# A hybrid decoder layer on one core: conditioning chunks and sample outputs in quarters of TensorE's array, another order of the first loads, and multiplies of unused data at the start

## The chip, the cores and the metric

The kernel runs on one core of a Trainium2 chip. The metric is the device time of one execution in microseconds, as the median of several runs. The core has a matrix engine (TensorE, PE in the rows; PEld is its weight load), VectorE (DVE), ScalarE (ACT), GpSimd (POOL) and SyncE (SP), and 16 DMA engines that serve queues. Each engine runs its own instructions in the order in which they stand in the program and waits on semaphores for the others.

## The reference

One decoder layer works on a prompt of 1024 tokens and on 8 samples of 4 tokens each, 1024 features, all in fp32. What matters here are three parts of it (shortened):

```python
mod = silu(c) @ ada_w + ada_b             # c: 9 vectors (1 prompt, 8 samples); ada_w 1024 x 6144
sh1, sc1, gt1, sh2, sc2, gt2 = split(mod, 6)
h = rmsnorm(x, norm1_g) * (1 + sc1) + sh1
u = h @ w_in                              # projections of all branches
...
# GLA branch, four heads, each with a state S of 128 x 256 per sequence
att = einsum('bhik,bhjk,bhijk->bhij', q, k, decay)
o = einsum('bhij,bhjv->bhiv', att, v) + einsum('bhik,bhkv->bhiv', q * exp(bc), S)
...
x = x + gt1 * (m @ w_out)                 # then the FFN, with sh2, sc2, gt2
```

The conditioning vectors `mod` scale and shift the normed inputs and gate the sums. They are needed for 9 sequences only, but their matrix has 6 million weights (24 MB).

## The kernel before

Activations lie transposed, features on the 128 partitions and tokens along the free axis. The work goes in two halves: half A has 512 prompt tokens, half B the other 512 and the 32 sample tokens. Every projection is done as three fp32r matmuls per 128 features of depth (`gemm`, L358 to L360): weights and activations are split into a high and a low part, and high x high, high x low, low x high are summed. So each weight tile of 512 KB is loaded by SP into a raw buffer and split by a cast on ScalarE and a subtraction on VectorE (`load_w`, L125 and L126), with three raw and three split buffers. The list scheduler of the framework decides at build time in which order each engine gets its instructions; it follows the order of the code, priorities, and the releases of pool buffers. A pool named `S` of 17 buffers holds whole activations and loads, two PSUM banks (`ax`) serve small results, six the projections.

The conditioning matrix is worked off in 12 chunks of 512 columns (`cc`), each of four loads of 512 KB, two depth tiles of 128 features in each. Its stationary operand is the activated conditioning matrix `cth`, which has 9 used columns of 32. Chunks 2 and 0 give the scale and shift of the first four feature tiles, chunks 3 and 1 those of the others, chunks 4 to 11 are needed later.

Chunks 2, 0, 3 and 1 go through `ada_first`: fp32 matmuls of 32 output columns, each to one of four groups of 32 output partitions (`g`, L178); a copy of the result (`row`, L181); and four matmuls by a selection matrix `sel`, which add the four groups and transpose them (L184). An fp32 matmul is recorded as two, one for each of its passes. 2 and 0 stand after the sum of squares of the first norm (`nps`, L365) and the spread of its result over the partitions (`rps`, L377). 3 and 1 stand between the halves of the norm, after the projection `lrps` and four projections `early20` to `early25` have done their first four feature tiles.

Chunks 4 to 11 go through `ada_chunk`: loads by `load_w` with the split, 16 fp32r matmuls on the full array (L226) whose stationary operand `cst` has the high part in columns 0 to 8 and the low part in 32 to 40 (`ada_split`, with the tile `zz`), a copy of 41 rows, four transposes of 41 columns (L198), two VectorE operations that add the parts. They are woven into the projections of half A up to about 500 us.

In half B each of four GLA heads computes the output of the samples, `pos`: eight fp32 matmuls (one per sample, L751) and one of the attention within the samples (L752) are summed in output partitions 0 to 31, copied to `osb`, turned by two transposes, and copied by ScalarE into the output tile.

Names that recur: `atta` is the product of attention weights (VectorE, L602) from the PSUM tile `dpsa`; `rpsoa` spreads a norm over partitions (L377); `rpsa`, `kpsa`, `vpsa`, `qpsa` are projections of half A.

Of the kernel before, what the change touches and what calls it, by code (L numbers as in the profile page):

```python
# [11 lines left out]
OP = mybir.AluOpType  # L12
PSUM = bass.MemoryType.PSUM
# [33 lines left out]
def hybrid_layer(ctx, tc, I, O):  # L47
# [42 lines left out]
    pool.dma_start(lmask, I["lmask"])  # L90
    bmask = cp.tile([P, NB], F32, name="bmask")
    pool.dma_start(bmask, I["bmask"])
    sel = cp.tile([P, 9], F32, name="sel")
    pool.dma_start(sel, I["sel"])
    hlru0 = cp.tile([P, NR, NB], F32, name="hlru0")
    pool.dma_start(hlru0, I["slru"])
    sconv = cp.tile([P, NR, NB, 3], F32, name="sconv")
    pool.dma_start(sconv, I["sconv"])
# [70 lines left out]
    def ada_first(cc):  # L169

        ps = ax(f"adaps{cc}")
        for kk in range(4):
            raw = S(f"ada{cc}{kk}")
            sp.dma_start(raw[:, :1024], I["ada_w"][cc, kk])
            for i in range(2):
                kt = 2 * kk + i
                g = 32 * (kt % 4)
                pe.matmul(ps[g:g + 32, :], cth[:, kt, :], raw[:, i * 512:(i + 1) * 512], start=(kt < 4), stop=(kt >= 4))  # L178
            yield 1.0
# [3 lines left out]
        for i in range(4):  # L183
            pe.matmul(tps[:, i * 16:i * 16 + 9], row[:, i * P:(i + 1) * P], sel, start=True, stop=True)  # L184
        mo = mod[:, 4 * cc:4 * cc + 4, :]
        dve.scalar_tensor_tensor(mo, tps[:, :64].rearrange("p (j m) -> p j m", m=16)[:, :, 0:9], 0.5, ada_bias(cc),
                                 op0=OP.mult, op1=OP.add)
        ada_derive(cc, mo)
        yield 1.0

    def ada_bias(cc):
        return bc(vec[:, V_ADAB + 4 * cc:V_ADAB + 4 * cc + 4].unsqueeze(2), [P, 4, 9])

    def ada_out(cc, ps, tps, row):
        n = 41
        act.activation(row[:n, :512], ps[:n], AF.Copy)
        for i in range(4):
            pe.transpose(tps[:, i * 64:i * 64 + n], row[:n, i * P:(i + 1) * P], ident[:n, :n])  # L198
        t3 = tps[:, :256].rearrange("p (j m) -> p j m", m=64)
        mo = mod[:, 4 * cc:4 * cc + 4, :]  # L200
        dve.scalar_tensor_tensor(mo, t3[:, :, 0:9], 0.5, ada_bias(cc), op0=OP.mult, op1=OP.add)
        dve.scalar_tensor_tensor(mo, t3[:, :, 32:41], 0.5, mo, op0=OP.mult, op1=OP.add)
        ada_derive(cc, mo)


    cst = []

    def ada_split():
        zz = S("zz")
        pool.memset(zz, 0.0)  # L210
        cw = S("cst", F32R)
        dve.tensor_copy(cw, zz)
        c3 = cw[:, :KD * P].rearrange("p (k m) -> p k m", m=P)
        dve.tensor_copy(c3[:, :, 0:9], cth[:, :, 0:9])
        dve.tensor_sub(c3[:, :, 32:41], cth[:, :, 0:9], c3[:, :, 0:9].bitcast(F32))
        cst.extend(c3[:, i, :] for i in range(KD))

    def ada_chunk(cc):

        ps = ax(f"adaps{cc}")  # L220
        for kk in range(4):
            w = load_w(I["ada_w"][cc, kk], 1024, f"ada{cc}{kk}")
            for i in range(2):
                kt = 2 * kk + i
                for u in range(2):
                    pe.matmul(ps, cst[kt], w[:, u, i * 512:(i + 1) * 512], start=(kt == 0 and u == 0),  # L226
                              stop=(kt == KD - 1 and u == 1))
            yield 0.87
        yield 0.5
        ada_out(cc, ps, ax(f"adat{cc}"), T(f"adar{cc}"))  # L230
# [89 lines left out]
    class Half:  # L320
# [129 lines left out]
        def norm1(s):  # L450
            box = s.rb1
            s.h = []
            for q in range(2):
                if s.hf == 0 and q:
                    s.lr_half(0)
                    for i, t in enumerate((T_Q, T_Q + 1, T_K, T_K + 1)):
# [4 lines left out]
                    for cc in (3, 1):  # L461
                        yield from ada_first(cc)
# [102 lines left out]
        def gla(s, pr, z, q, k, vg, vts):  # L565
# [125 lines left out]
            for i in range(2):  # L691
# [33 lines left out]
                if s.hf:  # L725
# [39 lines left out]
                    for v in range(2):  # L765
                        pe.transpose(pot[:, v * NS:(v + 1) * NS], osb[:, v * P:(v + 1) * P], ident[:NS, :NS])
# [494 lines left out]
```

## Time and profile before

| | us |
|---|---|
| median of three runs | 2069.88 (2068.68 to 2071.18) |
| profiled execution, its own time | 2071.19 |
| its span, from first to last instruction | 2069.4 |
| TensorE busy in the span | 2022.4 |
| VectorE busy | 1132.5 |
| ScalarE busy | 831.5 |
| mean granted TensorE clock (1 is 2.4 GHz) | 0.993 |

The span ends with the last instruction; 1.8 us of the profiled execution lie outside it. The table by stages says how much of a stretch each engine was busy. In a timeline each row is a run of equal operations; the number in brackets is the engine's idle time ahead of it and what ended that.

### The profile page before, as it was taken

The page shows a single profiled execution, that of the slowest core. Times are in us where ns is not written, and L with a number is a line of the kernel's source. Part 1 is how long each engine was busy: PE and PEld are TensorE (multiplying, and loading weights), DVE is VectorE, ACT ScalarE, POOL GpSimd, SP SyncE. Part 2 cuts the span into 40 slices and gives each one's busy share as a digit, 9 for nine tenths or more (in the row PEclk, how much of TensorE's full clock was granted, in tenths as well). Part 3 has the DMA queues.
Part 4 walks back from the last instruction along what each step waited for, and adds up shares of the span by engine and source line. Part 5 has one row for each costly group of instructions (what it writes and reads, how often), then busy time and mean ns, then how long its engine had stood idle before and what let it go on. Part 6 is the DMA issues. An engine that isn't in the chain of part 4 may idle for free. (4 is left out here: it accounts for less than half of the span.)

```text
span 2069.4 us, 31495 instructions
## 1 busy us (share of the span) xinstructions
PE 2022.4 (98%) x13106; PEld 1835.9 (89%) x13106; DVE 1132.5 (55%) x1795; ACT 831.5 (40%) x1153; POOL 85.3 (4%) x136
## 2 busy tenths in 40 slices
PE   6999999999999999999999999999999999999997
PEld 4787887788899888888899898899999999999997
DVE  4757767655347433446564597684243673333356
ACT  3536456645235322233352345563232442212232
POOL 1101001000000000000010011110000000000000
PEclk9999999999999999999999999999999999999999
DMA  7233423433344423342422313322233542232234
GB/s 284 79 111 94 138 76 116 134 122 110 98 154 148 133 79 105 102 139 72 152 69 85 115 48 105 107 78 96 79 96 99 166 136 94 75 107 86 90 114 126
DMA packets 74270, 228.39 MB, mean 110 GB/s; under 512 B 8496, under 2 KB 16304, under 8 KB 74128
## 3 DMA queue, kind: packets, MB, share of 16 engines
q1 hardware_dynamic: 70960, 216.98, 32.6%
q0 software_dynamic: 2624, 8.85, 1.2%
q8 instruction: 103, 1.69, 0.3%
q10 hardware_dynamic: 544, 0.56, 0.1%
q14 instruction: 39, 0.32, 0.0%
HBM read 217.12 MB, written 9.23 MB: 109 GB/s over the span
## 5 line engine op out<-in xcount | busy, mean ns | idle before, releaser
L360 PE MATMUL f3psb<-fab,f3b_hl 128*128 128x272 f32 x352 | 101.4, 288 | 0.0
L358 PE MATMUL f3psb<-fab,f3b_hl 128*128 128x272 f32 x352 | 101.3, 288 | 0.0
L359 PE MATMUL f3psb<-fab,f3b_hl 128*128 128x272 f32 x352 | 100.9, 287 | 0.0
L125 ACT ACTIVATE f3b_hl<-f3b_raw 128x768 fp32r<-128x768 f32 (+1 forms) x45 | 35.7, 793 | 88.4 <-PE f3psb L360 56.1
L358 PE MATMUL f3psa<-faa,f3a_hl 128*128 128x512 f32 x176 | 68.7, 390 | 0.0
L360 PE MATMUL f3psa<-faa,f3a_hl 128*128 128x512 f32 x176 | 68.5, 389 | 0.0
L359 PE MATMUL f3psa<-faa,f3a_hl 128*128 128x512 f32 x176 | 68.5, 389 | 0.0
L358 PEld LDWEIGHTS f3psb<-fab,f3b_hl 128*128 128x128 f32 x352 | 66.4, 189 | 0.0
L360 PEld LDWEIGHTS f3psb<-fab,f3b_hl 128*128 128x128 f32 x352 | 66.2, 188 | 0.0
L359 PEld LDWEIGHTS f3psb<-fab,f3b_hl 128*128 128x128 f32 x352 | 66.1, 188 | 0.0
L126 DVE TENSOR_TENSOR f3b_hl<-f3b_raw,f3b_hl 128x768 fp32r<-128x768 f32 (+1 forms) x45 | 40.1, 892 | 35.1 <-ACT f3b_hl L125 34.9
L125 ACT ACTIVATE f3a_hl<-f3a_raw 128x768 fp32r<-128x768 f32 (+1 forms) x32 | 25.4, 793 | 84.2 <-PE f3psa L360 46.4
L126 DVE TENSOR_TENSOR ada_hl<-ada_raw,ada_hl 128x1024 fp32r<-128x1024 f32 x32 | 38.9, 1222 | 24.8 <-ACT ada_hl L125 24.6
L126 DVE TENSOR_TENSOR f3a_hl<-f3a_raw,f3a_hl 128x768 fp32r<-128x768 f32 (+1 forms) x32 | 28.5, 890 | 39.0 <-ACT f3a_hl L125 38.3
L125 ACT ACTIVATE ada_hl<-ada_raw 128x1024 fp32r<-128x1024 f32 x32 | 33.5, 1054 | 35.6 <-PE vpsa L360 13.1
L358 PE MATMUL uxpsb<-h1b,uxpsb_hl 128*128 128x272 f32 x160 | 47.4, 296 | 0.0
L360 PE MATMUL uxpsb<-h1b,uxpsb_hl 128*128 128x272 f32 x160 | 46.2, 289 | 0.0
L358 PE MATMUL ugpsb<-h1b,ugpsb_hl 128*128 128x272 f32 x160 | 46.2, 289 | 0.0
L359 PE MATMUL uxpsb<-h1b,uxpsb_hl 128*128 128x272 f32 x160 | 46.1, 288 | 0.0
L360 PE MATMUL ugpsb<-h1b,ugpsb_hl 128*128 128x272 f32 x160 | 46.0, 288 | 0.0
L359 PE MATMUL ugpsb<-h1b,ugpsb_hl 128*128 128x272 f32 x160 | 45.8, 286 | 0.0
L360 PEld LDWEIGHTS f3psa<-faa,f3a_hl 128*128 128x128 f32 x176 | 33.0, 188 | 7.1 <-DVE f3a_hl L126 0.2
(1491 smaller groups left out, 7248.5 us busy)
## 6 DMA issues: line engine op xcount, KB each, us to landing
ada_raw<-in_ada_w SPq DMA_DIRECT2D x32, 512.0 KB, 3.6
f3b_raw<-in_ffn SPq DMA_DIRECT2D x23, 384.0 KB, 3.1
ada<-in_ada_w SPq DMA_DIRECT2D x16, 512.0 KB, 10.0
f3b_raw<-in_ffn SPq DMA_DIRECT2D x22, 320.0 KB, 2.9
woa_raw<-in_w_out SPq DMA_DIRECT2D x13, 512.0 KB, 3.4
wob_raw<-in_w_out SPq DMA_DIRECT2D x13, 512.0 KB, 3.3
f3a_raw<-in_ffn SPq DMA_DIRECT2D x16, 384.0 KB, 3.1
uxpsa_raw<-in_w_in SPq DMA_DIRECT2D x10, 512.0 KB, 3.6
```

The lines of the kernel that those rows point to most:

```text
L125: act.activation(hl[:, 0, :n], raw[:, :n], AF.Copy)
L126: dve.tensor_sub(hl[:, 1, :n], raw[:, :n], hl[:, 0, :n].bitcast(F32))
L358: pe.matmul(out, wh, x[:, o:o + w], start=st, stop=False)
L359: pe.matmul(out, wh, x[:, N + o:N + o + w], start=False, stop=False)
L360: pe.matmul(out, wl, x[:, o:o + w], start=False, stop=en)
```

## The change

All 12 chunks now go through one `ada_chunk`. A chunk is done in two halves of two loads; in each, four fp32 matmuls go to the four groups of output partitions, one depth tile each. The loads go straight into buffers of the pool `S`, with no split. The row copy has 128 rows, four full 128x128 transposes by the identity follow, and a VectorE reduction adds the four groups. `sel`, `zz`, `cst` and `ada_split` are gone.

The sample output `pos` is written in the same way: sample `b` goes to group `b % 4`, the attention part to group 96 to 127; `osb` has 128 rows, the two transposes are 128x128, and a VectorE reduction takes the place of ScalarE's last copy.

The loads of the masks and states (`lmask` 224 KB, `bmask` 4, `hlru` 40, `sconv` 120) leave GpSimd's queue at the start and stand in SP's queue after `early25`; the load of `sel` (4.5 KB) is gone. The loads of chunk 3 move ahead of `early24`, those of chunk 1 ahead of the matmuls of chunk 3. The function `occupy` multiplies unused data: ten fp32 matmuls of 128x512 zeros (set by a GpSimd memset) before the first norm's sums, and single ones around chunks 2 and 0.

```diff
-    pool.dma_start(lmask, I["lmask"])
-    pool.dma_start(bmask, I["bmask"])
-    pool.dma_start(sel, I["sel"])
-    pool.dma_start(hlru0, I["slru"])
-    pool.dma_start(sconv, I["sconv"])
+    def load_later():
+        for t, src in (lmask, "lmask"), (bmask, "bmask"), (hlru0, "slru"), (sconv, "sconv"):
+            sp.dma_start(t, I[src])
...
+    def groups(t, n):
+        return t.rearrange("p (j g m) -> p j m g", g=4, m=32)[:, :, 0:n, :]
...
+    def ada_chunk(cc, raws=None):
+        ps = ax(f"adaps{cc}")
+        for kk in range(0, 4, 2):
+            two = raws[kk:kk + 2] if raws else ada_load(cc, kk, kk + 2)
+            for g in range(4):
+                pe.matmul(ps[32 * g:32 * g + 32, :], cth[:, 2 * kk + g, :], two[g // 2][:, (g % 2) * 512:(g % 2 + 1) * 512],
+                          start=(kk == 0), stop=(kk == 2))
             yield 1.0
         row = T(f"adar{cc}")
         act.activation(row[:, :512], ps, AF.Copy)
         tps = ax(f"adat{cc}")
         for i in range(4):
-            pe.matmul(tps[:, i * 16:i * 16 + 9], row[:, i * P:(i + 1) * P], sel, start=True, stop=True)
+            pe.transpose(tps[:, i * P:(i + 1) * P], row[:, i * P:(i + 1) * P], ident)
         mo = mod[:, 4 * cc:4 * cc + 4, :]
+        dve.tensor_reduce(mo, groups(tps, 9), axis=AX.X, op=OP.add)
...
+                        if i == 2:
+                            a3 = ada_load(3, 0, 4)
...
-                    for cc in (3, 1):
-                        yield from ada_first(cc)
+                    a1 = ada_load(1, 0, 4)
+                    yield from ada_chunk(3, a3)
+                    yield from ada_chunk(1, a1)
...
                     for b in range(NB):
-                        pe.matmul(pos[:NS, :256], qm[:, b, :], sts[b // 4][:, (b % 4) * 256:(b % 4 + 1) * 256], start=(b == 0), stop=False)
-                    pe.matmul(pos[:NS, :256], atts[:, i * NS:(i + 1) * NS], vs[0], start=False, stop=True)
+                        g = 32 * (b % 4)
+                        pe.matmul(pos[g:g + 32, :256], qm[:, b, :], sts[b // 4][:, (b % 4) * 256:(b % 4 + 1) * 256], start=(b < 4),
+                                  stop=(3 < b < 7), skip_group_check=True)
+                    pe.matmul(pos[96:128, :256], atts[:, i * NS:(i + 1) * NS], vs[0], start=False, stop=True, skip_group_check=True)
...
-                        pe.transpose(pot[:, v * NS:(v + 1) * NS], osb[:, v * P:(v + 1) * P], ident[:NS, :NS])
-                    act.activation(o3[:, :, HP:], pot[:, :2 * NS].rearrange("p (v j) -> p v j", v=2), AF.Copy)
+                        pe.transpose(pot[:, v * P:(v + 1) * P], osb[:, v * P:(v + 1) * P], ident)
+                    dve.tensor_reduce(o3[:, :, HP:], groups(pot[:, :256], NS), axis=AX.X, op=OP.add)
...
+    zero = S("zero")
+    pool.memset(zero, 0.0)
+    idle = mm("idle")[:, 0]
+    def occupy(src, n):
+        for _ in range(n):
+            pe.matmul(idle, src[:, :P], src[:, :512], start=True, stop=True, skip_group_check=True)
+    occupy(zero, 10)
     A.load_x()
-    drain(A.norm1_sum())
-    drain(ada_first(2))
-    drain(ada_first(0))
+    a2, a0 = ada_load(2, 0, 4), ada_load(0, 0, 4)
+    sums = A.norm1_sum()
+    next(sums)
+    drain(ada_chunk(2, a2))
+    occupy(a2[3], 1)
+    drain(sums)
+    occupy(a0[1], 1)
+    drain(ada_chunk(0, a0))
+    occupy(a0[3], 2)
     drain(A.norm1())
-    ada_split()
+    load_later()
```

The scheduler then gives the engines new orders. Each row below is a run of equal instructions with its line, output and inputs.

TensorE at the start of the program, before (`ada20` to `ada23` are the four loads of chunk 2, `adat2` its turned result):

```order
L365 MATMUL nps1a_147<-ones_93,acc1a_117 128x1 x4
L365 MATMUL nps1a_147<-ones_93,sq1a7_145 128x1 x4
L377 MATMUL rps1a_170<-ident_80,rstd1a_156 128x128 x4
L178 MATMUL adaps2_177<-ada20_178,cth_107 32x512 x2
L178 MATMUL adaps2_177<-ada21_182,cth_107 32x512 x2
L178 MATMUL adaps2_177<-ada22_186,cth_107 32x512 x2
L178 MATMUL adaps2_177<-ada23_190,cth_107 32x512 x2
L184 MATMUL adat2_196<-sel_86,adar2_194 128x9 x4
L178 MATMUL adaps0_203<-ada00_204,cth_107 32x512 x2
L178 MATMUL adaps0_203<-ada01_208,cth_107 32x512 x2
L178 MATMUL adaps0_203<-ada02_212,cth_107 32x512 x2
L178 MATMUL adaps0_203<-ada03_216,cth_107 32x512 x2
```

and after:

```order
L1116 MATMUL idle_113<-zero_111 128x512 x10
L334 MATMUL nps1a_170<-ones_87,acc1a_124 128x1 x4
L334 MATMUL nps1a_170<-ones_87,sq1a7_152 128x1 x4
L186 MATMUL adaps2_193<-ada20_154,cth_101 32x512 x2
L186 MATMUL adaps2_193<-ada21_156,cth_101 32x512 x2
L186 MATMUL adaps2_193<-ada22_158,cth_101 32x512 x2
L186 MATMUL adaps2_193<-ada23_160,cth_101 32x512 x2
L1116 MATMUL idle_113<-ada23_160 128x512
L193 MATMUL adat2_204<-ident_80,adar2_202 128x128 x4
L346 MATMUL rps1a_213<-ident_80,rstd1a_179 128x128 x4
L186 MATMUL adaps0_221<-ada00_162,cth_101 32x512 x2
L1116 MATMUL idle_113<-ada01_164 128x512
```

The multiplies of unused data stand first, chunk 2 stands ahead of the spread `rps1a`, and single multiplies stand inside chunk 0 and (in the rows that follow) before and behind its transposes. The projection `lrpsa` follows as it did.

TensorE where chunk 5 begins, among projections of half A, before:

```order
L360 MATMUL vpsa101_1081<-h1a1_236,vpsa101_hl_1084 128x512
L198 MATMUL adat4_1030<-ident_80,adar4_1031 128x41 x4
L226 MATMUL adaps5_1040<-ada50_hl_1043,cst_410 128x512 x4
L705 MATMUL upsa000_1054<-va00_527,kta0_619 128x256
L358 MATMUL vpsa101_1081<-h1a2_241,vpsa101_hl_1084 128x512
L359 MATMUL vpsa101_1081<-h1a2_241,vpsa101_hl_1084 128x512
L360 MATMUL vpsa101_1081<-h1a2_241,vpsa101_hl_1084 128x512
```

and after:

```order
L186 MATMUL adaps5_946<-ada50_947,cth_101 32x512 x2
L620 MATMUL spsa02_955<-wa02_877 128x64 x5
L186 MATMUL adaps5_946<-ada51_949,cth_101 32x512 x2
L620 MATMUL spsa02_955<-wa02_877 128x64 x3
L328 MATMUL kpsa11_967<-h1a5_410,kpsa11_hl_970 128x512
L329 MATMUL kpsa11_967<-h1a5_410,kpsa11_hl_970 128x512
```

Before, the four matmuls of a load form one piece. After, the two of a load stand alone here, with five matmuls of another product between them and the next two. The eight chunks form 17 such pieces: four of two matmuls in chunk 4; two, two and four in chunks 5 and 6; eight at once in 7, 9 and 11; four and four in 8 and 10. The loads of chunk 4 stand in SP's queue between those of the projections `vpsa`. In `pos`, three heads have two pieces, four matmuls and then four with the attention part; one head has one.

VectorE around 175 to 190 us, where TensorE has its longest wait in mid-program, for the product `atta1` of the tile `dpsa11` (`kea1`, `wa` and `oa` are products of the attention, `rpsa1_hl` the split of a weight), before:

```order
L588 TENSOR_TENSOR kea1_1301<-bca1_1226 128x1024
L602 TENSOR_TENSOR atta1_1307<-dpsa10_1308,ident_80 128x512
L126 TENSOR_TENSOR rpsa1_hl_1409<-rpsa1_raw_1407,rpsa1_hl_1409 128x1024
L632 TENSOR_TENSOR wa164_1396<-bca1_1226 128x8x64
L633 TENSOR_TENSOR wa164_1396<-bca1_1226 128x8x64
L795 TENSOR_TENSOR oa00_1128<-oa00_1128,rboa00_1319 128x1024
L602 TENSOR_TENSOR atta1_1307<-dpsa11_1322,ident_80 128x512
```

and after:

```order
L195 TENSOR_REDUCE mod_98<-adat6_1301 128x36
L560 TENSOR_TENSOR kea1_1311<-bca1_1235 128x1024
L196 SCALAR_TENSOR_TENSOR mod_98<-mod_98,vec_78 128x36
L574 TENSOR_TENSOR atta1_1317<-dpsa10_1318,ident_80 128x512
L209 TENSOR_TENSOR shd_100<-mod_98 128x32
L125 TENSOR_TENSOR rpsa2_hl_1483<-rpsa2_raw_1481,rpsa2_hl_1483 128x1024
L769 TENSOR_TENSOR oa00_1138<-oa00_1138,rboa00_1329 128x1024
L574 TENSOR_TENSOR atta1_1317<-dpsa11_1332,ident_80 128x512
```

Before, four operations stand between the two products `atta1`; after, the first of them stands behind the reduction of chunk 6 and `kea1`, and three stand between the two. On TensorE the second spread, `rpsoa01`, waited for the second `atta1`; now it waits for ScalarE's copy of the first spread `rpsoa00`, which waits for the reduction, and `dpsa11` behind them waits for the first `atta1`. Three projection matmuls lie between `rpsoa00` and `dpsa11`.

## Rows read from the trace of the kernel before

**Rows 1.** The page's first part: busy us, share of the span, instructions.

```profile
PE 2022.4 (98%) x13106; PEld 1835.9 (89%) x13106; DVE 1132.5 (55%) x1795; ACT 831.5 (40%) x1153; POOL 85.3 (4%) x136
```

**Rows 2.** Table by stages: us, busy us by engine, PEclk, DMA, GB/s.

```profile
0.00:60.00 60.00, 38.03 (x184) 25.42 (x185) 27.16 (x79) 19.83 (x30) 5.86 (x17) 0.93 0.71 259
...
190.00:520.00 330.00, 330.00 (x1529) 267.46 (x1528) 216.74 (x293) 183.23 (x241) 18.55 (x29) 0.99 0.36 115
```

**Rows 3.** TensorE's waits: who waits for whom, us in total, times, longest.

```profile
PE nps1a L365 <- DVE lw L270: 13.5, 1, 13.5
```

**Rows 4.** Timeline of PE, the start: start us, us, operation [idle before].

```profile
13.51 1.84 PE L365 MATMUL nps1a<-ones,acc1a 128*128 128x1 f32 x8 [13.51 <-DVE lw L270]
...
19.27 2.07 PE L377 MATMUL rps1a<-ident,rstd1a 128*128 128x128 f32 x8 [2.22 <-DVE rstd1a L289]
21.27 3.31 PE L178 MATMUL adaps<-ada,cth 128*32 128x512 f32 x16
...
26.33 1.92 PE L178 MATMUL adaps<-ada,cth 128*32 128x512 f32 x16
...
32.06 0.77 PE L479 MATMUL lrpsa<-h1a,lr_hla 128*128 128x512 f32 x1 [2.00 <-DVE lr_hla L474]
```

**Rows 5.** Table by stages, of four short stretches.

```profile
13.00:17.00 4.00, 3.50 (x16) 3.49 (x16) 0.61 (x3) 0.00 (x0) 0.00 (x0) 1.00 1.03 415
34.00:36.00 2.00, 2.00 (x6) 1.54 (x5) 2.00 (x3) 1.28 (x3) 0.00 (x0) 0.50 0.67 252
38.00:40.00 2.00, 2.00 (x11) 1.64 (x10) 0.84 (x1) 1.06 (x1) 0.00 (x0) 1.00 0.72 258
188.00:195.00 7.00, 6.41 (x22) 5.49 (x22) 6.00 (x9) 3.28 (x6) 0.19 (x1) 0.51 0.07 5
```

**Rows 6.** Timeline of the other engines, the start.

```profile
1.98 0.56 POOL L90 DMA_DIRECT2D lmask<-in_lmask  x1
...
12.68 0.68 DVE L393 TENSOR_TENSOR acc1a<-acc1a,sq1a 128x512 f32<-128x512 f32 x1
...
28.31 1.00 POOL L210 MEMSET zz<- 128x1088 f32 x1 [22.85 <-PE adaps L178]
```

**Rows 7.** Timeline of PE, chunks 3 and 1.

```profile
47.71 1.92 PE L178 MATMUL adaps<-ada,cth 128*32 128x512 f32 x16
...
53.55 1.05 PE L178 MATMUL adaps<-ada,cth 128*32 128x512 f32 x4 [0.23 <-DMA ada<-in_ada_w]
...
57.41 0.50 PE L479 MATMUL lrpsa<-h1a,lr_hla 128*128 128x512 f32 x1 [1.04 <-ACT h1a L430]
```

**Rows 8.** Timeline of PE, four matmuls of chunk 4 and what follows.

```profile
106.22 1.07 PE L226 MATMUL adaps<-ada_hl,cst 128*128 128x512 f32 x4
107.13 1.89 PE L648 MATMUL spsa<-wa 128*128 128x64 f32 x16
```

**Rows 9.** Timeline of PE, the sample output of one head.

```profile
1137.80 0.29 PE L358 MATMUL vpsb<-h1b,vpsb_hl 128*128 128x272 f32 x1
1137.92 0.29 PE L359 MATMUL vpsb<-h1b,vpsb_hl 128*128 128x272 f32 x1
1138.14 3.64 PE L751 MATMUL posb<-s0b,qmb 128*32 128x256 f32 x16
1141.71 0.61 PE L752 MATMUL posb<-vs,attsb 32*32 32x256 f32 x2
1142.26 0.50 PE L758 MATMUL uptb<-vr,kemb 128*128 128x256 f32 x2
```

**Rows 10.** The page's sixth part: DMA issues, KB each, us to landing.

```profile
ada_raw<-in_ada_w SPq DMA_DIRECT2D x32, 512.0 KB, 3.6
```

**Rows 11.** Timeline of PE, the stall before the spread.

```profile
188.59 2.08 PE L377 MATMUL rpsoa<-ident,orstda 128*128 128x128 f32 x8 [3.72 <-DVE atta L602]
```

**Rows 12.** Timeline of DVE, the product that the spread waits for.

```profile
187.86 0.68 DVE L602 TENSOR_TENSOR atta<-dpsa,ident 128x512 f32<-128x512 f32 x1
```

**Rows 13.** Operations on the tile `adaps`: weight loads, ns min/median/max.

```profile
L178 PEld LDWEIGHTS adaps<-ada,cth x64: 106/109/178, 21.3 to 53.6; 128*32 128x32 f32 x64
```

## What I predict

> **What bounds the kernel now.** I read the busy table of the page first. TensorE (PE) is busy for 2022.4 us, 98% of the span [rows 1], so a microsecond counts only if it comes off TensorE or out of one of its few idle stretches. Next the table by stages [rows 2]: the first 60 us hold 38.03 us of TensorE work, so 22 are idle there, while 190 to 520 us are full, 330.00 of 330. Then TensorE's waits: the list is headed by 13.5 us before its first matmul [rows 3], and the longest in mid-program is the 3.72 us of part 4. Last come the timelines of three places that the diff touches: the start, a conditioning chunk, a sample output. The profiled execution took 2071.19 us, 1.8 us more than its span of 2069.4 and 1.3 us above the median of 2069.88. I sum against 2071.2 and give the result on the median's basis.
>
> **Part 1, the start.** Before, the first matmul stands at 13.51 us, the first two chunks at 21.27 and 26.33, and the first projection (`lrpsa`) at 32.06 [rows 4]. The chunk at 21.27 takes 3.31 us, that at 26.33 takes 1.92, with the same 16 records: four steps each, in which four groups run side by side, of 0.85 us the first time and 0.43 the second, after some 7 us of scattered work. Later the granted clock itself shows the two levels: 0.50 of 2.4 GHz, so 1.2 GHz, from 34 to 36 us, after 2.00 us of idling ahead of 32.06, and 1.00 from 38 us; the engine does 6 matmuls in 2 us at the one and 11 at the other [rows 5].
>
> After, ten fp32 128x512 multiplies of zeros stand first, as soon as GpSimd has cleared their tile. Five issues of 0.56 us are gone from its queue, ahead of its memsets at 4.7, and a memset like that of `zz`, 1.00 us, is new [rows 6]: about 3.7 us. Such a multiply takes two passes, each as long as a step above, so twenty passes take 8.6 to 17.1 us. I take 11, a slow beginning and the rest fast; they end near 15.
>
> The squares of the norm, summed by 13.36 before [rows 6], should be there near 12.5: 392 KB of other loads no longer share the DMA engines with the inputs, about 1 us at the 415 GB/s of the stretch behind [rows 5]. So the fillers hold TensorE, to 15. Then the sums take 1.8 us at the high clock (3.5 before, two records of 1.84 that overlap by a part), chunk 2 1.8, a filler 0.87, transposes 0.5, the spread 1.1 (2.07 before), chunk 0 1.8 and its filler 0.87, with about 0.5 of waiting for the row copy: chunk 0 ends near 24.2, where it ended at 28.25. From there to the first projection lie 3.8 us before; the copy, the transposes and the modulation stay, a reduction of some 0.2 us joins them, and the weight loads of the transposes run at one clock, so I take 3.5, which gives 27.7 instead of 32.06: -4.4.
>
> The slow stretch behind goes too, as two fillers stand in that gap. From 32.06 to 37.86 TensorE does 13 matmuls in 5.8 us, at 0.23 each they are 3.0: -2.8. Behind the early projections stand chunks 3 and 1, from 47.71 to 57.41, where TensorE idles for 0.23 us before 53.55 and 1.04 before 57.41 [rows 7], and for two row copies. After, the loads of chunk 3 are issued ahead of `early24`, and its matmuls are threaded through that projection, whose work covers its row copy; chunk 1's copy stays bare. I count -1.3, the two gaps of the rows; without that cover it is 0. Sum of the start: **-8.5**, bounds -5 (fillers slow for longer) and -11 (fillers all fast; then the last quarter of chunk 0, which lands at about 21.3, is late next). The four mask and state loads, moved to SP's queue behind `early25` and ahead of one weight load, take about 1 us of transfer; TensorE is then busy with the early projections, so 0, and 1 us if that load is waited for.
>
> **Part 2, chunks 4 to 11.** Before, 8 chunks of 16 matmuls on the full array; four take 0.91 us (106.22 to 107.13 [rows 8]), so 0.227 each and 29.1 us in all. After, a chunk has 8 fp32 multiplies, to four groups of output partitions in turn. A full set of four takes two steps of 0.43. Two alone also take two steps: the pair at 53.55 is 1.05 us, two steps and the tail of a record [rows 7]. So it matters where the scheduler splits them. In the new order the eight chunks stand in 17 unbroken pieces (four pairs in chunk 4; pair, pair, four in 5 and in 6; fours or eights in the rest): 8+6+6+4+4+4+4+4 = 40 steps, 17.4 us. Each piece is entered from the full array and left to it. At a sample output such a switch shows: matmuls 0.125 apart are followed after 0.22, and 16 passes of 0.216 end 0.11 late [rows 9]; so 0.1 us a switch, 17 x 2 x 0.1 = 3.4. Together 20.8 against 29.1: **-8.3**, bounds -4.9 (0.2 a switch) and -11.7 (none).
>
> The casts of the 32 loads (ScalarE and VectorE) go too; TensorE has no idle time in 190 to 520 us that they could have caused, so 0 there (the one stall earlier is part 4). Four transposes of 41 columns become four of 128, both bound by weight loads of the same array; the added reduction replaces an addition on VectorE; 0 each, hidden by projections, and about 0.3 us a chunk if they were bare. What the casts gave was slack: a load now goes straight to the array. From issue to landing it takes 3.6 us [rows 10], and it is issued when a buffer of the shared pool comes free, mostly 35 to 100 TensorE instructions (7 us and up) ahead of use. SP issues in order, so `vpsa110` and others queue behind a waiting load, and TensorE behind them. I take **+1**, near the covered end, with bounds 0 and +8.
>
> **Part 3, sample outputs.** Before, one head takes from 1138.05 to 1142.26, 16 serial passes of 0.216, two more, and three switches, 4.2 us [rows 9]; four heads 16.8. After, eight multiplies go to four groups: 4 passes, 0.87, then the last one in group 96 with its own switch, 0.52, and two switches a piece of 0.2: 1.78 a head, 7.1 in all (the order splits three heads in two pieces, which is inside the bound). **-9.7**, bounds -8 and -10.5. The copy is of 128 rows at the same width, and ScalarE goes by the width; one short operation moves from ScalarE to VectorE, beside the projections: 0, and 0.2 a head if bare.
>
> **Part 4, the stall before 188.59.** TensorE waits 3.72 us [rows 11] for the `atta` product of `dpsa11`, which VectorE runs at 187.86 [rows 12], behind a split, two `wa` products and one of `oa`; the clock then is 0.51 for 7 us [rows 5], which costs some 3.4 us. Total 7.1. After, `rpsoa01` waits for ScalarE's copy of `rpsoa00` instead, and that and `dpsa11` wait earlier: for the reduction of `adat6`, and for the `atta` of `dpsa10`, ahead of which VectorE has the reduction, `kea` and a small operation. That is about 0.2 + 1.2 + 0.2 + 0.68 = 2.3 us, of which a spread of 0.9 and three projections of 0.23 cover 1.6; with the wait for the reduction itself 1 to 1.5 us of idling in two pieces. The gaps that the low clock followed were 2.00 [rows 4] and 3.72, so I count no slow stretch. **-4**, short of the full 7.1 - 1.5, since other work of VectorE comes nearer too; bounds 0 (as now) and -7.
>
> **Sum.** -8.5 - 8.3 - 9.7 - 4 + 1 = -29.5. 2071.2 - 29.5 = 2041.7, on the median's basis 2040.4. I say 2041.
>
> **Rivals.**
> 1. The fillers run slow throughout and only delay the sums: they end at 20.8, and the first projection follows 5.8 us later than above, at 33.5, which is 1.4 behind the old one; with the clock still low the sums and chunk 2 take their old 3.5 and 3.3 us, 3.2 more. The start is then +5 instead of -8.5: 2041.7 + 13.5 = 2055. For: the chunk at 21.27 was still slow 8 us after the first matmul. Against: that work was scattered, the fillers are not. Chance 0.12.
> 2. Slower than before: ada loads are waited for at the 17 pieces, since buffers come free only as other work ends. At a full transfer of 3.6 us each the cost is 61, so 2103. It decides from 29.5 / 17 = 1.7 us each. For: SP's order. Against: the 7 us of distance, and a DMA share of 0.36 in that stage [rows 2]. Chance 0.04; smaller waits lie in the upper range.
> 3. Pieces cost more than their steps: the array empties, and the four weight loads of a piece, 0.11 to 0.18 us each [rows 13], stand bare ahead of it, up to 0.7 us. With 17 + 7 pieces that is 17 more: 2059. For: 0.1 us is what shows at one place only. Against: in rows 9 the block of 16 records starts with 0.1 us of delay, weight load and all. Chance 0.08. The Trainium skill, page TensorEngine Tiling (Array Packing), section Key Properties, says that a change of tiling mode drains TensorE, which speaks against this split; it gives no price, and the trace agrees with the 0.1 us above.
> 4. More waits of TensorE for VectorE and ScalarE go in the half with the samples, with the slow stretches behind them, 10 us: 2031. For: stage 1100 to 1400 has such waits, and one operation a head leaves ScalarE. Against: the casts that go lie long ahead of it. Chance 0.12.
> 5. Nothing arrives at the end, since what is freed is waited for by something else: 2070. TensorE's 98% speaks against it. Chance 0.02.
>
> **How the numbers follow.** Forecast 0.62, its own range 2033 to 2049; the rivals 0.12, 0.04, 0.08, 0.12 and 0.02. The range goes from rival 4 to rival 1, 2031 to 2056, and leaves out rivals 2, 3 and 5 and small tails. Within 0.2% (4 us, what a measurement of this kernel can tell from no change) is rival 5, 0.02; slower is rival 2, 0.04; faster the rest, 0.94.
>
> **What would show it.** The first projection near 27.7 and no slow matmuls behind it; sets of four in chunks 4 to 11 of 0.87 us, 20.8 in total; a sample head in 1.8 us; no wait of 3.7 us for `atta`; waits for ada loads of about 1 us together. The prediction is wrong if TensorE's list of waits has several lines of transfers, if the first projection starts behind 30 us, or if new idle time in other stages exceeds 5 us.

## The result, and the profile after

The changed kernel takes 2044.1 us (median, 2043.49 to 2046.31), the kernel before 2070.53 us in the same comparison: a ratio of 0.9875, interval 0.9858 to 0.9893. That is 26.4 us less; 29.5 were forecast. The profiled execution is the slowest of the four, 2046.31 us with a span of 2044.3. The busy table of its page answers [rows 1]:

```profile
PE 2013.5 (98%) x13118; PEld 1811.1 (89%) x13118; DVE 1097.1 (54%) x1768; ACT 799.2 (39%) x1117; POOL 79.5 (4%) x131
```

The ledger below compares the start of the same work in TensorE's two timelines. It shows in which stage the time went in these two profiles.

| TensorE starts | before, us | after, us | difference | gained in the stage |
|---|---|---|---|---|
| the first `lrpsa` | 32.06 | 28.67 | -3.4 | 3.4 |
| the last `lrpsa` | 62.30 | 58.76 | -3.5 | 0.1 |
| the first `papsa` (all chunks done) | 502.88 | 487.77 | -15.1 | 11.6 |
| the first `f3psa` | 767.75 | 751.59 | -16.2 | 1.1 |
| the first `posb` | 1138.14 | 1122.02 | -16.1 | 0 |
| the first `gbpsb` (all sample outputs done) | 1344.29 | 1319.01 | -25.3 | 9.2 |
| the last `rps3b` | 2061.56 | 2036.44 | -25.1 | -0.2 |

**The start.** TensorE's timeline after, where [rows 4] and [rows 7] stood before (start us, us, operation, count, idle ahead):

```profile
3.63 11.84 PE L1116 MATMUL idle<-zero 128*128 128x512 f32 x20 [3.63 <-POOL rmask L104]
15.30 0.95 PE L334 MATMUL nps1a<-ones,acc1a 128*128 128x1 f32 x8
...
17.07 1.92 PE L186 MATMUL adaps<-ada,cth 128*32 128x512 f32 x16
...
25.19 1.13 PE L1116 MATMUL idle<-ada 128*128 128x512 f32 x2
...
26.59 1.02 PE L1116 MATMUL idle<-ada 128*128 128x512 f32 x2
28.67 0.50 PE L451 MATMUL lrpsa<-h1a,lr_hla 128*128 128x512 f32 x1 [1.06 <-ACT h1a L399]
29.01 0.40 PE L327 MATMUL early<-h1a,early_hl 128*128 128x512 f32 x1
30.02 0.70 PE L452 MATMUL lrpsa<-h1a,lr_hla 128*128 128x512 f32 x1 [0.61 <-DVE h1a L400]
...
48.34 0.66 PE L193 MATMUL adat<-ident,adar 128*128 128x128 f32 x4 [0.77 <-ACT adar L190]
...
51.56 0.66 PE L193 MATMUL adat<-ident,adar 128*128 128x128 f32 x4 [0.72 <-ACT adar L190]
54.14 0.80 PE L451 MATMUL lrpsa<-h1a,lr_hla 128*128 128x512 f32 x1 [1.92 <-ACT h1a L399]
```

and two stretches of its table by stages (us, busy us of PE, PEld, DVE, ACT, POOL, PEclk, DMA share, GB/s):

```profile
26.00:27.60 1.60, 1.60 (x7) 0.73 (x6) 0.81 (x2) 1.60 (x2) 0.00 (x0) 1.00 1.03 412
30.00:33.50 3.50, 3.48 (x8) 2.75 (x9) 3.09 (x4) 1.54 (x4) 0.00 (x0) 0.52 0.83 312
```

The fillers (`idle`) begin at 3.63 and last 11.7 us, and the sums behind them run at full speed, 0.95 where a row of eight took 1.84. The multiplies behind chunk 0 end at 27.6. Then come two gaps of 1.06 and 0.61 us with two matmuls between them, and behind these the granted clock is 0.52, with 8 matmuls in 3.5 us, as it was before ([rows 5], 34 to 36 us). The wait ahead of 54.14 is 1.92 us; it was 1.04.

**The chunks.** Here stand a piece of two matmuls (four records, two passes each) and a piece of eight, in place of [rows 8]; then TensorE's waits from 62 to 520 us, in place of [rows 11]:

```profile
106.23 0.39 PE L329 MATMUL qpsa<-h1a,qpsa_hl 128*128 128x512 f32 x1
106.46 0.39 PE L327 MATMUL qpsa<-h1a,qpsa_hl 128*128 128x512 f32 x1
106.78 1.05 PE L186 MATMUL adaps<-ada,cth 128*32 128x512 f32 x4
107.76 1.33 PE L620 MATMUL spsa<-wa 128*128 128x64 f32 x10
```

```profile
215.25 0.39 PE L329 MATMUL rpsa<-h1a,rpsa_hl 128*128 128x512 f32 x1
215.57 1.92 PE L186 MATMUL adaps<-ada,cth 128*32 128x512 f32 x16
217.43 0.77 PE L620 MATMUL spsa<-wa 128*128 128x64 f32 x5
```

```profile
PE spsa L620 <- DVE mod L195: 1.5, 1, 1.5
PE rpsoa L346 <- ACT rboa L349: 0.7, 1, 0.7
```

Two matmuls take 0.98 us (106.78 to 107.76), eight take 1.86. The entrance (start to start from the matmul before) takes 0.32 us where 0.23 is usual, the exit 0.12 to 0.14 beyond the steps of 0.43. No transfer is in this list of waits, and instead of 3.72 us TensorE waits 0.7 and 1.5.

**The sample outputs.** The first head, in place of [rows 9]:

```profile
1121.80 0.29 PE L328 MATMUL vpsb<-h1b,vpsb_hl 128*128 128x272 f32 x1
1122.02 0.64 PE L724 MATMUL posb<-s0b,qmb 128*32 128x256 f32 x8
1122.59 0.51 PE L732 MATMUL uptb<-vr,kemb 128*128 128x256 f32 x2
...
1123.77 0.64 PE L724 MATMUL posb<-s0b,qmb 128*32 128x256 f32 x8
1124.34 0.61 PE L726 MATMUL posb<-vs,attsb 32*32 32x256 f32 x2
1124.88 0.50 PE L732 MATMUL uptb<-vr,kemb 128*128 128x256 f32 x2
```

Eight records of `posb` (four matmuls) fill 0.57 us; 16 took 3.57 before. The head takes 0.57 and 1.11 us in its two pieces and 0.09 to enter each.

### The profile page after: what moved, and what is told of

Same layout as the page of the kernel before. It is cut to its first block, busy times and chain, and to the rows that moved or that the text cites. A ratio compares the mean times of both kernels' runs of the same rounds, so it can differ in the third digit from the quotient of the medians.

```text
span 2044.3 us, 31396 instructions
## 1 busy us (share of the span) xinstructions
PE 2013.5 (98%) x13118; PEld 1811.1 (89%) x13118; DVE 1097.1 (54%) x1768; ACT 799.2 (39%) x1117; POOL 79.5 (4%) x131
## 5 line engine op out<-in xcount | busy, mean ns | idle before, releaser
L329 PEld LDWEIGHTS f3psa<-faa,f3a_hl 128*128 128x128 f32 x176 | 33.0, 188 | 7.1 <-DVE f3a_hl L125 0.2
L328 PEld LDWEIGHTS f3psa<-faa,f3a_hl 128*128 128x128 f32 x176 | 33.1, 188 | 6.9
L327 PEld LDWEIGHTS f3psa<-faa,f3a_hl 128*128 128x128 f32 x176 | 33.1, 188 | 6.6
```

The source lines that it names most:

```text
L327: pe.matmul(out, wh, x[:, o:o + w], start=st, stop=False)
L328: pe.matmul(out, wh, x[:, N + o:N + o + w], start=False, stop=False)
L329: pe.matmul(out, wl, x[:, o:o + w], start=False, stop=en)
```

## The experiments

Theory A throughout: TensorE sets the time, so a part brings what it takes off TensorE; the start falls short since its gaps stay. The rivals are named in each expectation. Every kernel was timed beside the kernel before; the table gives the ratio to it, and the difference from the changed kernel worked out as the difference of the ratios times 2071 us. Each ratio has an interval of 3 to 4 us to each side, so a difference of two is uncertain by some 5 us, and what is smaller is read from traces only.

| kernel | ratio to before | interval | against the changed kernel, us |
|---|---|---|---|
| changed kernel | 0.9875 | 0.9858 to 0.9893 | |
| the same again | 0.9878 | 0.9861 to 0.9894 | +0.6 |
| start_old | 0.9893 | 0.9877 to 0.9910 | +3.7 |
| pos_serial | 0.9921 | 0.9906 to 0.9936 | +9.5 |
| chunks_full | 0.9923 | 0.9908 to 0.9937 | +9.9 |
| casts_back | 0.9945 | 0.9930 to 0.9960 | +14.5 |
| one_group | 1.0052 | 1.0037 to 1.0067 | +36.7 |
| no_fill | 0.9861 | 0.9846 to 0.9876 | -2.9 |
| fill_gap | 0.9874 | 0.9859 to 0.9889 | -0.2 |
| start_fit | 0.9869 | 0.9852 to 0.9885 | -1.2 |
| eights | 0.9827 | 0.9812 to 0.9841 | -9.9 |
| eights_nofill | 0.9836 | 0.9821 to 0.9851 | -8.1 |
| eights_gap2 | 0.9833 | 0.9818 to 0.9848 | -8.7 |

### One part undone

**start_old**: the start of the kernel before, with the quarters everywhere else.

```diff
...
-    drain(ada_chunk(2, a2))
-    occupy(a2[3], 1)
...
+    drain(A.norm1_sum())
+    drain(ada_first(2))
+    drain(ada_first(0))
...
```

> The changed kernel with the start of the kernel before: chunks 2, 0, 3, 1 through the selection matrix, loads in the old order, no multiplies of unused data; chunks 4 to 11 and sample outputs in quarters. Theory A (the start brought what the traces show at the projection lrpsa, 32.06 to 28.67 us, and nothing behind it): 3.3 us more than the changed kernel, about 2047.4. Theory B (the earlier loads also pay behind 70 us): 6 us more or above, 2050.

Measured: 2049.8 us, 3.7 more by the ratios. That is A's size, but within the noise of two ratios, so B's 6 isn't excluded. In its profile the first `papsa` starts at 491.70 us, 3.9 later than in the profile after and 5.6 later than in *again* below; so the start is worth some 4 to 6 us there.

**pos_serial**: the sample outputs in one group of output partitions.

```diff
-                        pe.matmul(pos[g:g + 32, :256], qm[:, b, :], sts[b // 4][:, (b % 4) * 256:(b % 4 + 1) * 256], start=(b < 4),
-                                  stop=(3 < b < 7), skip_group_check=True)
+                        pe.matmul(pos[:NS, :256], qm[:, b, :], sts[b // 4][:, (b % 4) * 256:(b % 4 + 1) * 256], start=(b == 0), stop=False)
...
```

> The changed kernel with the sample outputs summed in one group of 32 output partitions as before. Theory A (four groups run side by side, and TensorE sets the time there): four heads of 4.2 us instead of 1.8, 9.3 us more, about 2053.4. Theory B (the heads lie beside waits for VectorE, which eat the gain): less than 5 us more, under 2049.

Measured: 2056.52 us, 9.5 more (three executions at 2056.1 to 2056.9, one at 2051.67). From the first `posb` to the first `gbpsb` its profile takes 207.2 us, the profile after 197.0. The gain of the heads is TensorE's own time; theory A.

**chunks_full**: chunks 4 to 11 with split loads, on the full array.

```diff
-            yield from ada_chunk(cc)
+            yield from ada_full(cc)
...
+            w = load_w(I["ada_w"][cc, kk], 1024, f"ada{cc}{kk}")
...
+                    pe.matmul(ps, cst[kt], w[:, u, i * 512:(i + 1) * 512], start=(kt == 0 and u == 0),
+                              stop=(kt == KD - 1 and u == 1))
...
```

> The changed kernel with chunks 4 to 11 as before: split loads, 16 matmuls on the full array. Theory A (the gain is the array's time, 29.1 against 21.0 us, and the stall near 188 us with its slow clock comes back, 3 to 4 us): 11 to 12 us more, about 2055.5. Theory B (the array's time is hidden, only the stall counts): 4 us more, 2048.

Measured: 2055.01 us, 9.9 more. From the last `lrpsa` to the first `papsa` it takes 440.3 us, the changed kernel 429.0: 11.3 more, and the wait is the old one:

```profile
PE rpsoa L382 <- DVE atta L610: 3.7, 1, 3.7
```

The array's time and the stall account for it; theory A, against B's 4 us.

**one_group**: the unsplit loads, but the eight matmuls one after the other into partitions 0 to 31.

```diff
-                pe.matmul(ps[32 * g:32 * g + 32, :], cth[:, 2 * kk + g, :], two[g // 2][:, (g % 2) * 512:(g % 2 + 1) * 512],
+                o = 0 if cc > 3 else 32 * g
+                pe.matmul(ps[o:o + 32, :], cth[:, 2 * kk + g, :], two[g // 2][:, (g % 2) * 512:(g % 2 + 1) * 512],
...
```

> The changed kernel with chunks 4 to 11 multiplied by the same unsplit loads, but all eight matmuls summed in output partitions 0 to 31, one after the other. Theory A (the gain of the quarters is that four run side by side): 16 passes of 0.43 us a chunk, 55 in all and 13 pieces with 0.2 of switches, 58 against 21.0: 36 us more, about 2080, slower than before. Theory B (the gain is that 32 columns are cheap or the casts are gone): 8 us more or less, 2052.

Measured: 2080.75 us, 36.7 more than the changed kernel and slower than the kernel before. One chunk in TensorE's timeline, to be set beside the 1.92 us at 215.57:

```profile
198.14 7.05 PE L187 MATMUL adaps<-ada,cth 128*32 128x512 f32 x16 [0.25 <-DVE atta L579]
205.13 0.50 PE L332 MATMUL rpsa<-h1a,rpsa_hl 128*128 128x512 f32 x1
```

The same 16 records take 6.99 us instead of 1.86. Doing without the split would lose; that four groups run side by side pays for it.

**casts_back**: the quarters as they are, with the split of each load done too and its result unused.

```diff
+            if cc > 3:
+                for raw in two:
+                    hl = wp.tile([P, 2, 1024], F32R, tag="hl", name=f"unused{cc}{kk}", bufs=3)
+                    with tc.high_priority(AHEAD):
+                        act.activation(hl[:, 0, :], raw[:, :1024], AF.Copy)
+                        dve.tensor_sub(hl[:, 1, :], raw[:, :1024], hl[:, 0, :].bitcast(F32))
```

> The changed kernel with the split of the 32 loads of chunks 4 to 11 done all the same (ScalarE and VectorE, 72 us of work), its result unused; the chunks themselves stay in quarters. Theory A (the gain of the chunks is the array's time): 0 to 4 us more, the latter if the stall near 188 us comes back, 2044 to 2048. Theory B (the gain is the relief of ScalarE and VectorE): 8 us more or above, over 2052.

Measured: 2060.38 us, 14.5 more: B's number. Its waits, and two stretches of the table by stages (us, as above):

```profile
PE rpsa L333 <- ACT rpsa_hl L124: 3.8, 1, 3.8
PE rpsa L335 <- DVE rpsa_hl L125: 3.2, 2, 2.9
```

```profile
180.00:190.00 10.00, 10.00 (x65) 8.67 (x64) 9.66 (x19) 5.80 (x8) 3.05 (x2) 1.00 0.22 89
190.00:210.00 20.00, 13.29 (x52) 8.61 (x52) 18.99 (x20) 11.40 (x14) 2.80 (x2) 0.74 0.33 110
```

VectorE is busy for 18.99 of 20 us from 190 to 210, TensorE waits 7.0 us for weight splits that stand behind the unused ones, and the clock of that stretch is 0.74 on average. The unused splits also pass through the three split buffers of the projections, so the run doesn't tell the engines' time from the wait for a buffer. The prediction's 0 for the casts doesn't hold at the pace of the changed kernel. Before, the 32 splits were spread over some 400 us (chunks_full has the same splits at that pace and only the one wait); the quarters are done by 250 us, and at that pace the 72 us of splits didn't fit beside the attention. The chunks could be packed so closely only without them. Quarters with the splits at the old pace weren't tried, so how much of B holds at that pace is open.

### The start

**again**: the changed kernel itself.

> The changed kernel itself a second time. Theory A (whether the clock falls in the gap ahead of 30 us differs from one execution to the next, and with it 2 to 3 us): median 2044, executions spread over 2 to 3 us; where the profile shows no slow matmuls from 30 to 33.5 us its second part of the first norm starts near 51.8 instead of 54.1 us. Theory B (every execution has that slow stretch): executions within 1 us, 54.1.

Measured: 2044.85 us (2043.73 to 2045.42). In this profile the fillers take 10.2 us and the slow stretch is missing behind the same two gaps:

```profile
27.21 0.50 PE L451 MATMUL lrpsa<-h1a,lr_hla 128*128 128x512 f32 x1 [1.06 <-ACT h1a L399]
...
28.55 0.50 PE L452 MATMUL lrpsa<-h1a,lr_hla 128*128 128x512 f32 x1 [0.61 <-DVE h1a L400]
28.89 0.40 PE L451 MATMUL lrpsa<-h1a,lr_hla 128*128 128x512 f32 x1
```

```profile
30.00:33.50 3.50, 3.50 (x17) 2.81 (x17) 1.63 (x3) 0.91 (x1) 0.00 (x0) 1.00 0.97 341
52.00:54.00 2.00, 2.00 (x6) 1.51 (x6) 1.83 (x3) 0.90 (x2) 0.00 (x0) 0.50 0.00 0
```

The clock is 1.00 from 30 to 33.5 us, 17 matmuls instead of 8 there; the second part starts at 51.11 us, and the last `lrpsa` at 55.77, 6.5 us earlier than before and not 3.5. Of these 3 us half stand ahead of the first projection, where fewer fillers ran slow, and half behind it, where the slow stretch is missing. So whether the clock falls in these gaps differs between executions of one program; theory A. Of the seven profiles with this start, two show it (the profile after and *pos_serial*). In this profile one chunk load came late:

```profile
PE adaps L186 <- DMA ada<-in_ada_w: 0.3, 1, 0.3
```

It stands in the middle of a set of four at 223.20, which took 2.32 instead of 1.00 us. The profile after is of the slowest of its four executions, by 1.8 to 2.8 us, this one of the fastest.

**fill_gap**: two more multiplies of unused data in that gap.

```diff
-    occupy(a0[3], 2)
+    occupy(a0[3], 4)
```

> The changed kernel with two more multiplies of unused data between chunk 0 and the first projection, 1.9 us in a gap of 2.4. Theory A (the clock falls there in some executions, since TensorE has only one matmul between 27.6 and 30.0 us): no slow matmul behind 30 us, executions within 1 us of each other, 2043 or a little less. Theory B (the clock falls for another reason): slow matmuls from 30 to 33.5 us as before, 0 to 1 us more.

Measured: 2045.43 us (2045.06 to 2046.07), no gain. Its profile has the full clock from 26 to 36 us and 51.82 for the second part, as the luckier executions of the changed kernel have. That agrees with A, but it doesn't show that these multiplies held the clock, and the time doesn't tell them from none.

**no_fill**: no multiplies of unused data.

```diff
...
-    occupy(zero, 10)
...
-    occupy(a2[3], 1)
...
-    occupy(a0[1], 1)
...
-    occupy(a0[3], 2)
...
```

> The changed kernel without any multiply of unused data. Theory A (the fillers are worth the clock, but hold the sums for 2 to 3 us, so the two nearly cancel): sums at 12.6 us at the low clock, first projection near 28.5, the slow stretch behind it in every execution: 0 to 3 us more than the changed kernel, 2044 to 2047. Theory B (they only delay): 3 us less, 2041. Theory C (they are what the start gains): 5 us more, 2049.

Measured: 2043.58 us, 2.9 less by the ratios, which is within the noise of two of them. Its start:

```profile
12.85 1.84 PE L334 MATMUL nps1a<-ones,acc1a 128*128 128x1 f32 x8 [12.85 <-DVE lw L239]
...
16.32 3.64 PE L186 MATMUL adaps<-ada,cth 128*32 128x512 f32 x16
...
22.18 1.92 PE L186 MATMUL adaps<-ada,cth 128*32 128x512 f32 x16
...
27.73 0.77 PE L451 MATMUL lrpsa<-h1a,lr_hla 128*128 128x512 f32 x1 [2.22 <-DVE lr_hla L446]
...
36.69 1.92 PE L186 MATMUL adaps<-ada,cth 128*32 128x512 f32 x16
...
50.23 0.50 PE L451 MATMUL lrpsa<-h1a,lr_hla 128*128 128x512 f32 x1 [1.92 <-ACT h1a L399]
```

Sums and chunk 2 are slow here, 1.84 and 3.64, and lose 3.5 us; but they begin 2.5 us earlier. Chunk 0 ends at 24.1 us without fillers, and with them at 25.2 in the profile after and 23.7 in *again*; the first projection follows 3.5 to 3.6 us later in all three. No gain of the fillers by themselves can be measured. They even move the plan: in every kernel here that has them ahead of the first projection, the scheduler breaks chunk 3 into three pieces (38.66, 40.30 and 46.51 us in the profile after), the last behind the early projections; without them it stands in one piece at 36.69 and its copy is covered. The second part of the norm starts 22.5 us behind the first projection here, 23.9 in *again*.

**start_fit**: seven multiplies at the beginning, two more in the gap, chunk 1 ahead of chunk 3's transposes, two multiplies behind chunk 1.

```diff
-                    yield from ada_chunk(3, a3)
-                    yield from ada_chunk(1, a1)
+                    g3, g1 = ada_chunk(3, a3), ada_chunk(1, a1)
+                    for g in g3, g3, g1, g1:
+                        next(g)
+                    drain(g3)
+                    drain(g1)
+                    occupy(a1[3], 2)
+                    yield 2.0
...
-    occupy(zero, 10)
+    occupy(zero, 7)
...
-    occupy(a0[3], 2)
+    occupy(a0[3], 4)
```

> The changed kernel with 7 instead of 10 multiplies at the beginning, two more in the gap ahead of the first projection, chunk 1 multiplied ahead of the transposes of chunk 3, and two multiplies behind it. Theory A (TensorE sets the time of the start): sums near 12.9 us, the last load of chunk 0 (20.2 us) late next, first projection near 26, no copy wait of 0.8 us, no slow stretch behind 54 us: 4 to 5 us less than the changed kernel, about 2039.5. Theory B (the loads set it): 1 to 2 us less, 2042.5.

Measured: 2045.36 us, 1.2 less by the ratios: B's size and within the noise, and no transfer is among TensorE's waits at the start, as B would have it. The sums start at 12.39 us as A wants, but chunk 2 then takes 3.28, most of it at the low clock, and the first projection is at 27.61. The last `lrpsa` is at 55.22, so the end of the start is no better than in *again*. What sets the first projection in all these variants (27.2 to 28.7) is the end of chunk 0 near 24 to 25 us and a chain of some 3.5 us behind it on ScalarE and VectorE, which more or fewer fillers don't shorten.

### The pieces

**eights**: each chunk's four loads asked for first, its eight matmuls in one piece.

```diff
-            yield from ada_chunk(cc)
+            raws = ada_load(cc, 0, 4)
+            yield 0.0
+            g = ada_chunk(cc, raws)
+            next(g)
+            next(g)
+            yield 2.0
+            yield from g
```

> The changed kernel with the four loads of a chunk asked for first and its eight matmuls in one unbroken piece, in chunks 4 to 11. Theory A (a pair takes the same two steps as a set of four, and each piece pays two switches): 32 steps instead of 40 and 8 pieces instead of 17, 8 x 1.95 = 15.6 us of TensorE instead of 21.0: 5.4 us less, about 2038.7. Theory B (a piece that needs four loads waits for the last of them): waits on transfers in TensorE's list, 0 to 2 us less.

Measured: 2035.02 us, a ratio of 0.9827: faster than both kernels. Its waits from 62 to 520 us are two, neither of them for a transfer:

```profile
PE rpsoa L352 <- ACT rboa L355: 0.7, 1, 0.7
PE adaps L186 <- DVE atta L580: 0.2, 1, 0.2
```

From the last `lrpsa` to the first `papsa` it takes 421.1 us instead of 429.0. Of these 7.9 us 4.6 are the pieces themselves (14.8 instead of 19.4), 0.8 are nine entrances fewer at 0.09, and 1.5 are the wait at `spsa` that has gone; 1.0 isn't traced. The first two make A's 5.4, and the wait comes on top.

**eights_nofill** and **eights_gap2**: the same without fillers, and with two behind chunk 1 only.

```diff
...
-    occupy(zero, 10)
...
+                    idle = ax("idle")
+                    for _ in range(2):
+                        pe.matmul(idle, a1[3][:, :P], a1[3][:, :512], start=True, stop=True, skip_group_check=True)
...
```

> The unbroken chunks together with no multiplies of unused data. Theory A (the two edits add up; without fillers the scheduler puts chunk 3 in one piece into an early projection, and the second part of the norm starts near 50): 2 us less than the unbroken chunks alone (2035.0), about 2033. Theory B (the fillers are needed once the chunks are short): 2035 to 2037.

> The same with two multiplies of unused data in one place only, behind chunk 1, in the gap of about 2 us ahead of the second part of the norm. Theory A (the slow stretch behind that gap, some 3.5 us at half speed, goes): 1.5 us less than without them, about 2031.5. Theory B (they delay the second part by what they save): the same time.

Measured: 2036.0 and 2035.42 us. Neither can be told from *eights*. That is B's time in both, but A's 2033 and 2031.5 are only 3 to 4 us away, so the times alone don't rule A out. In the first, the wait of 1.92 us ahead of 51.01 wasn't followed by a low clock, so there was nothing to save for the second in these profiles.

## Why the prediction was right, and where it was not

The forecast of 2041 was 3 us too low, within its own range of 2033 to 2049. It came right since three terms that make 22 of its 29.5 us held one by one; the 1.1 us that helped against the short start were not forecast, and they were luck. Its terms, in the order of its sum, against the profile:

| term | forecast, us | measured, us |
|---|---|---|
| start | -8.5 | -3.5 in the profile after, -6.5 in *again* |
| chunks 4 to 11 | -8.3 (20.8 left) | 21.0 left of 29.1: -8.1 |
| waits for loads | +1 | 0, and 1.3 in *again* |
| sample outputs | -9.7 (7.1 left) | 7.2 left of 16.8; -9.2 in the stage |
| stall before 188.59 | -4 | -3.5, what is left of the stage's 11.6; by its rows -4.9 |
| not in the sum | 0 | -1.1 between `papsa` and `f3psa` |

**Chunks.** The pieces of the new order are eight of two matmuls at 0.98 us, six of four at 1.00 and three of eight at 1.85, 19.4 us, and 17 entrances at 0.09 more, 1.6. That a pair costs as much as a set of four, read from one lone pair before [rows 7], was the step that made the sum right, and it was also the reserve: *eights* takes it. The Trainium skill, page TensorEngine Tiling (Array Packing), section Key Properties, says that a change of tiling mode drains TensorE. The trace agrees in that every switch takes time, 0.09 us to enter and 0.12 to 0.14 to leave. Rival 3, with up to 0.7 a piece, is out.

**Loads.** No chunk load stands among TensorE's waits in the profile after, and one of 0.3 us in *again*, so rival 2 is out. In *eights*, where a piece needs all four loads, there is none either. (The wait of 0.8 us for a state, `s0b`, ahead of a `posb` was there before, with 0.7.)

**Sample outputs.** Right in size and cause (*pos_serial*, 9.5).

**Stall.** The old wait went, and two short ones came, 0.7 at `rpsoa` as forecast and 1.5 at `spsa` (200.81 us), behind the reduction of a later chunk on VectorE, which wasn't. No low clock followed. Of the old 7.1 us that leaves a gain of 4.9; the ledger has 3.5 for it, as a remainder, and the 1.4 between the two isn't traced. The casts' 0 was read from the old pace (330.00 of 330 us busy [rows 2]); *casts_back* shows that at the new pace they would have cost 14.5 us.

**Start.** This term was too large: -8.5 against -3.5 and -6.5. Of its three parts the first was near: the fillers start at 3.63 (3.7 forecast) and take 11.7 us (11 forecast), and the first projection came 3.4 us earlier instead of 4.4. The second, 2.8 us for the slow stretch, rested on "two fillers stand in that gap". They stand ahead of it: they are done at 27.6, and TensorE then idles for 1.06 and 0.61 us. Part 4 of the prediction took 2.00 and 3.72 us for the only gaps that a low clock had followed. That was misread: before, it also followed the 1.04 us ahead of 57.41 [rows 7], as the table by stages of the kernel before shows:

```profile
57.00:60.00 3.00, 2.60 (x8) 2.03 (x9) 3.00 (x7) 2.19 (x4) 0.00 (x0) 0.71 0.00 0
60.00:62.00 2.00, 2.00 (x7) 1.59 (x6) 1.36 (x3) 0.00 (x0) 0.00 (x0) 0.58 0.00 0
```

So gaps of 1.06 and 0.61 us were not safe; after them the clock fell in the profile after and held in *again*. The third, 1.3 us, took the threading of chunk 3 through `early24` for cover of its copy. The order had its last matmuls (six records at 46.51) behind the projections, so the copy stayed bare (0.77), and the wait for `h1a` grew from 1.04 to 1.92: +0.7 instead of -1.3.

Rival 1 (slow fillers that delay) is half true: 7 of 20 passes were slow, and the fillers delayed the sums by 2.5 us (1.0 in *again*) and saved the clock; the two cancel within the noise (*no_fill*). Rival 4 isn't seen: in the half with the samples the stage of the heads gained 9.2 us and the rest lost 0.2. The 1.1 us between `papsa` and `f3psa` lie in half A, and 0.7 of them are a wait for ScalarE ahead of `f1psa` (647.99 us before) that the profile after doesn't have.

## What to carry to other kernels

Small stationary operands paid here when they stood side by side in all four groups of output partitions, in unbroken sets of four or more: a set cut in two cost the same again (0.98 us for two, 1.00 for four) plus two switches. When a preparing step on another engine is dropped, ask what pace it had allowed, since the work may now be packed where that step would not fit. Multiplies of unused data that lasted until the real work started went with full speed there (0.95 us for the sums), but they held that work up by 1.0 to 2.5 us; without a run that leaves them out, one can't say that they pay.

## What the runs showed of the hardware

The number of slow passes at the beginning differs between executions of one program: 7 of the 20 fillers' passes in the profile after, 4 in *again*, at 0.85 against 0.43 us, with PEclk given as 1.00 all the time. (With the same start in other kernels it is 7 in *pos_serial* and 4 to 6 in *chunks_full*, *casts_back*, *one_group* and *eights*.) The Trainium skill, page TensorE: Matmul & The Clock Gate, section Part 1, says that the number of slow matmuls at a kernel's start varies from run to run; these runs agree.

Gaps of 1.06 and 0.61 us with two matmuls between were followed by a clock of 0.52 in one execution and of 1.00 in another. That of 1.92 us ahead of the second part was followed by 0.5 to 0.6 in *again*, *no_fill* and *fill_gap*, and by 1.00 in *eights_nofill*. In the half with the samples a gap of 2.42 us ahead of 1195.82 was followed by 1.00 in the kernel before, and one of 2.30 us ahead of 1184.14 by 0.50 in the profile after. A single profile therefore says of such a gap what happened, not what it costs.
